# A float32 matmul with bias and residual: bias by a late VectorE shuffle, dense dummy products, finer last stores, and one store cut into 108 and 20 rows

## The chip, the cores and the metric

The kernel runs on one core of a Trainium2 chip. Times are device microseconds (us) of that core; where the text says "span", it means the time from the first to the last instruction in the profile, which is about 2 us shorter. Most runs agree within 0.3%, so a difference of a few tenths of a microsecond needs several rounds. The rounds were spread over five chips, so kernels of different rounds are best compared by their ratio to the kernel before, which ran beside them.

## The reference

```python
# x [16, 512, 1024], weight [1024, 768], bias [768], residual [16, 512, 768], all float32
def reference(x, weight, bias, residual):
    return (np.matmul(x, weight) + bias + residual).astype(np.float32)
```

The 8192 rows of x are 64 tiles of 128 rows. Eight tiles make a super tile, which is loaded and stored in transfers of up to 4 MB; a partition holds eight consecutive rows, so every transfer has long runs per partition. A whole transfer has 128 partitions; where this text speaks of the rows of a transfer, as in "a cut at row 108", it means these partitions. Altogether 87 MB cross the DMA queue.

## The kernel before

x is cast to bf16 on ScalarE, transposed on TensorE, copied out of PSUM by VectorE, multiplied, and added to the residual (to which GpSimd has already added the bias). One in-order queue on SyncE issues nearly all transfers, in the order of a list. These parts matter here (cut):

```python
WARM = 10
HEAD_ORDER = [('bias',), ('warm', 10), ('cast', 0, 'v'), ('cast', 1, 's'), ('tr', 0), ('tr', 1), ...]
ORDER = [('x', 0, 0, 2), ('w', 0, 0, 2), ('x', 0, 2, 4), ('w', 1, 0, 2), ('w', 2, 0, 2), ('w', 3, 0, 2),
 ('x', 0, 4, 6), ('x', 0, 6, 8), ('r', 0, 0, 5), ('x', 1, 0, 4), ('r', 0, 5, 8), ('r', 1, 0, 5),
 ('x', 1, 4, 8), ...                                   # x, w, r: loads; (kind, super tile, first, last)
 ('s', 4, 0, 8), ('s', 5, 0, 8), ('s', 6, 0, 8), ('s', 7, 0, 5), ('s', 7, 5, 7), ('s', 7, 7, 8)]   # stores
...
# a store: all 128 partitions, tiles j0 to j1
nc.sync.dma_start(out=out_d[S, :, j0:j1, :], in_=R[S % RO_SLOTS][:, j0:j1, :])
...
# the bias on all partitions: a product of a row of ones with the bias row, in fp32
nc.tensor.matmul(bias_ps[:, n0:n0 + nl], lhsT=ones_row, rhs=bias_row[:, n0:n0 + nl], ...)
nc.vector.tensor_copy(out=bias_sb, in_=bias_ps)
...
for t in range(HEAD, n_t):          # the steady loop
    cast(t + 2); transp(t + 1)      # ScalarE; TensorE and VectorE
    ... 16 products of tile t ...
    finish(t - 1)                   # VectorE: PSUM + residual
```

## Time and profile before

Three runs took 211.27, 211.29 and 211.53 us. The first lines of the profile's page: busy time of each engine with its share of the span, and what the DMA queues moved. PE stands for TensorE's matmuls, PEld for its weight loads, DVE for VectorE, ACT for ScalarE and POOL for GpSimd; x1308 is a count of instructions.

```profile
span 209.6 us, 3135 instructions
...
PE 204.3 (97%) x1308; PEld 133.6 (64%) x1308; DVE 104.7 (50%) x139; ACT 68.0 (32%) x68; POOL 114.6 (55%) x70
...
DMA packets 5200, 87.23 MB, mean 416 GB/s; under 512 B 577, under 2 KB 577, under 8 KB 1346
## 3 DMA queue, kind: packets, MB, share of 16 engines
q1 hardware_dynamic: 5184, 87.03, 97.6%
q8 instruction: 10, 0.16, 0.3%
```

Two things are full at once: PE (TensorE's matmuls) for 97% of the span, and the DMA queue q1, whose packets take 97.6% of the time of 16 DMA engines. The ten "instruction" packets of queue q8 are 0.3% of the DMA time.

The head, from the timeline (start, duration, engine, line, what, and in brackets the idle time before and what ended it):

```profile
3.30 2.92 PE L196 MATMUL psum_o<-bias_row,ones_row 1*128 1x512 f32 x4
...
5.53 1.04 ACT L131 CAST xb<-x_tile 128x1024 bf16<-128x1024 f32 x1 [2.78 <-DMA x_tile<-in_x_dram]
...
6.26 0.96 DVE L200 COPY bias_sb<-psum_o 128x768 f32<-128x768 f32 x1 [5.12 <-PE psum_o L196]
7.13 0.68 DVE L131 CAST xb<-x_tile 128x1024 bf16<-128x1024 f32 x1
...
10.82 2.11 PE L146 MATMUL psum_o<-w_sb,xt 128*128 128x512 bf16 x8
```

The fp32 bias products hold PE from 3.30 to 6.22 us, and the bias copy holds VectorE until 7.22, so the cast of tile 0 there starts only at 7.13 (the two records overlap by 0.09 us) though its x landed at 5.53. The first real product starts at 10.82.

ScalarE's casts of super tile 1 (tiles 8 to 11, then 12 to 14 in this window), and PE's transposes of tiles 8 and 12:

```profile
31.32 3.89 ACT L131 CAST xb<-x_tile 128x1024 bf16<-128x1024 f32 x4 [8.74 <-DMA x_tile<-in_x_dram]
43.61 2.94 ACT L131 CAST xb<-x_tile 128x1024 bf16<-128x1024 f32 x3 [8.41 <-DMA x_tile<-in_x_dram]
```

```profile
32.88 0.60 PE L139 MATMUL pt<-ident,xb 128*128 128x128 f32 x4
...
45.03 0.60 PE L139 MATMUL pt<-ident,xb 128*128 128x128 f32 x4
```

A cast takes 1.04 us. So tile 8 is ready at 32.36 and is transposed at 32.88; tile 12 is ready at 44.65 and is transposed at 45.03. From there on x is early.

The tail, as busy time in stretches. The last two columns are the mean share of busy DMA engines and what they moved.

```profile
core 0: us, PE busy (x) PEld busy (x) DVE busy (x) ACT busy (x) POOL busy (x), PEclk, DMA share, GB/s
194.00:197.00 3.00, 3.00 (x22) 1.96 (x21) 1.56 (x2) 0.00 (x0) 0.00 (x0) 1.00 1.03 440
197.00:200.00 3.00, 3.00 (x22) 1.96 (x21) 1.55 (x2) 0.00 (x0) 0.00 (x0) 1.00 0.52 217
200.00:203.00 3.00, 3.00 (x22) 1.96 (x21) 1.56 (x2) 0.00 (x0) 0.00 (x0) 1.00 0.98 415
203.00:206.00 3.00, 2.70 (x17) 1.41 (x15) 1.92 (x3) 0.00 (x0) 0.00 (x0) 1.00 0.77 323
```

PE ends at 205.70 us. The queue is not full here any more on average (217 GB/s at 197 to 200 us).

The trace also has a record of every DMA packet. A transfer of 128 rows leaves 16 packets of 4 bytes, one at the end of each engine's share (the semaphore; 578 in this trace), so one can see when each of the 16 engines was done. The records name no engine: where this text follows one, it goes by packets that start within 0.02 us of the end of another. For three transfers (worked out from these records, us):

```
transfer                  first engine done   last engine done   spread
x of tiles 6 and 7                    19.55              19.97     0.42
x of tiles 8 to 11                    29.03              30.79     1.76
store of super tile 6                197.09             200.82     3.74
```

A single engine is behind in the second line. At 20.89 us a 16 KB instruction packet takes 1.10 us, and the 15,360-byte packet that follows takes 1.04 instead of 0.58: 1.56 us lost on one engine. Such packets come every 20 us or so; when the spread grew again, from 2.53 to 3.73 us at about 177 us, one had again just gone by (176.63).

### The profile page before, as it was taken

The numbers are of one execution on the slowest core, as the hardware profiler recorded it, in microseconds if no ns is written. First come the engines' busy times: TensorE is split into PE (matmuls) and PEld (weight loads), VectorE is DVE, ScalarE is ACT, GpSimd is POOL, SyncE is SP. The second block draws the span as 40 slices with busy tenths as digits, with TensorE's granted clock in tenths as the row PEclk, the third lists the DMA queues.
The fourth block names the chain that finished last, engine by engine and source line by source line (L and its number), as shares of the span: only waits on it lengthen the run. The fifth ranks groups of instructions, "written<-read, shape, count | busy, mean of one in ns | idle before, by whom it ended". The sixth has DMA issues, their size and how long they took to land.

```text
span 209.6 us, 3135 instructions
## 1 busy us (share of the span) xinstructions
PE 204.3 (97%) x1308; PEld 133.6 (64%) x1308; DVE 104.7 (50%) x139; ACT 68.0 (32%) x68; POOL 114.6 (55%) x70
## 2 busy tenths in 40 slices
PE   7999999999999999999999999999999999999992
PEld 4756666666666666666666666666666666666661
DVE  0473643474375455455544554554455445545542
ACT  2445307060733053323432152330533134321000
POOL 1000099995278980199599702994059910799000
PEclk9999999999999999999999999999999999999999
DMA  6999999999999999999999999999999999999785
GB/s 236 425 434 436 427 403 448 456 406 404 462 450 402 417 441 425 421 458 400 436 458 422 425 403 436 446 441 419 427 427 446 425 413 435 432 419 441 336 379 231
DMA packets 5200, 87.23 MB, mean 416 GB/s; under 512 B 577, under 2 KB 577, under 8 KB 1346
## 3 DMA queue, kind: packets, MB, share of 16 engines
q1 hardware_dynamic: 5184, 87.03, 97.6%
q8 instruction: 10, 0.16, 0.3%
q14 instruction: 4, 0.03, 0.0%
q10 hardware_dynamic: 2, 0.00, 0.0%
HBM read 61.87 MB, written 25.17 MB: 415 GB/s over the span
## 4 chain that ended last, share of the span: by engine, by line
PE 97%; DVE 1%; issue 0%
PE psum_o L146 79%; PE pt L139 14%; PE psum_o L210 1%; PE psum_o L196 1%; PE psum_o L244 1%; PE psum_o L191 1%; DVE xt L140 0%; DVE ro L248 0%; DVE warm L185 0%
## 5 line engine op out<-in xcount | busy, mean ns | idle before, releaser
L146 PE MATMUL psum_o<-w_sb,xt 128*128 128x512 bf16 x1008 | 174.7, 327 | 0.3 <-DVE xt L140 0.3
L146 PEld LDWEIGHTS <-xt 128*128 128x128 bf16 x1008 | 98.8, 98 | 59.1 <-DVE xt L140 0.6
L171 POOL TENSOR_TENSOR ro<-ro,bias_sb 128x768 f32<-128x768 f32 x58 | 103.2, 1818 | 53.5 <-DMA ro<-in_residual_dram 53.5
L131 ACT CAST xb<-x_tile 128x1024 bf16<-128x1024 f32 x62 | 63.2, 1044 | 116.4 <-PE pt L139 58.6
L140 DVE COPY xt<-pt 128x1024 bf16<-128x1024 bf16 x64 | 44.1, 691 | 79.0 <-PE pt L139 78.9
L181 DVE TENSOR_TENSOR ro<-psum_o,ro 128x768 f32<-128x768 f32 x57 | 54.2, 950 | 12.0 <-POOL ro L171 10.9
L139 PE MATMUL pt<-ident,xb 128*128 128x128 f32 x256 | 39.0, 277 | 0.0
L139 PEld LDWEIGHTS pt<-ident,xb 128*128 128x128 f32 x256 | 30.7, 143 | 7.3
L167 POOL TENSOR_TENSOR ro<-ro 128x768 f32<-128x768 f32 x6 | 10.8, 1814 | 25.2 <-DMA ro<-in_residual_dram 25.2
L177 DVE TENSOR_TENSOR ro<-psum_o,bias_sb 128x768 f32<-128x768 f32 x6 | 5.6, 950 | 3.5 <-PE psum_o L146 3.5
L216 ACT CAST w_sb<-ro 128x768 bf16<-128x768 f32 x4 | 3.3, 832 | 3.8 <-DMA ro<-in_weight_dram 3.8
L200 DVE COPY bias_sb<-psum_o 128x768 f32<-128x768 f32 x1 | 1.0, 958 | 5.1 <-PE psum_o L196 5.1
L210 PE MATMUL psum_o<-warm 128*128 128x256 bf16 x14 | 3.4, 416 | 0.0
L191 PE MATMUL psum_o<-warm 128*128 128x256 bf16 x10 | 2.3, 418 | 1.1 <-DVE warm L185 1.1
L196 PE MATMUL psum_o<-bias_row,ones_row 1*128 1x512 f32 (+1 forms) x4 | 2.9, 880 | 0.0
L210 PEld LDWEIGHTS <-warm 128*128 128x128 bf16 x14 | 1.9, 142 | 1.4 <-issue 0.7
L244 PE MATMUL psum_o<-w_sb,xt 128*128 128x512 bf16 (+1 forms) x16 | 2.8, 326 | 0.0
L191 PEld LDWEIGHTS <-warm 128*128 128x128 bf16 x10 | 1.3, 144 | 1.5 <-DVE warm L185 1.1
L244 PEld LDWEIGHTS <-xt 128*128 128x128 bf16 x16 | 1.6, 98 | 1.1
L196 PEld LDWEIGHTS psum_o<-bias_row,ones_row 1*128 1x128 f32 x4 | 1.2, 318 | 1.5 <-issue 1.5
L216 DVE CAST w_sb<-ro 128x768 bf16<-128x768 f32 x4 | 2.0, 553 | 0.0
L188 ACT ACT_TABLE_LOAD x1 | 1.3, 1283 | 1.3 <-PEq L266 1.3
(12 smaller groups left out, 4.0 us busy)
## 6 DMA issues: line engine op xcount, KB each, us to landing
x_tile<-in_x_dram SPq DMA_DIRECT2D x6, 4096.0 KB, 29.8
out_dram<-ro SPq DMA_DIRECT2D x7, 3072.0 KB, 24.7
ro<-in_residual_dram SPq DMA_DIRECT2D x6, 3072.0 KB, 21.3
x_tile<-in_x_dram SPq DMA_DIRECT2D x4, 1024.0 KB, 8.2
x_tile<-in_x_dram SPq DMA_DIRECT2D x2, 2048.0 KB, 25.9
ro<-in_residual_dram SPq DMA_DIRECT2D x2, 1920.0 KB, 22.1
ro<-in_weight_dram SPq DMA_DIRECT2D x4, 768.0 KB, 10.2
ro<-in_residual_dram SPq DMA_DIRECT2D x2, 1152.0 KB, 28.6
```

The costliest lines, as they stand in the source:

```text
L131: K_((nc.scalar.copy if how == "s" else nc.vector.tensor_copy)(out=dst, in_=src))
L139: K_(nc.tensor.transpose(out=pt[:, q, :], in_=words[:, ts(q, P)], identity=ident))
L140: K_(nc.vector.tensor_copy(out=XT[t % XT_N].rearrange("p q m e -> p (q m e)"), in_=pt.rearrange("p q m -> p (q m)").bitcast(BF16),))
L146: K_(nc.tensor.matmul(PO[t % HEAD][:, n0:n0 + nl], lhsT=XT[t % XT_N][:, q, :, e], rhs=w_sb[:, q, e, n0:n0 + nl], start=(q == 0 and e == 0) ...
L167: K_(nc.gpsimd.tensor_add(out=r, in0=r, in1=tmp(t)))
L171: K_(nc.gpsimd.tensor_add(out=r, in0=r, in1=bias_sb))
L177: K_(nc.vector.tensor_add(out=tmp(t), in0=p, in1=bias_sb))
L181: K_(nc.vector.tensor_add(out=row(t), in0=p, in1=row(t)))
L191: K_(nc.tensor.matmul(PO[0][:, 0:256], lhsT=warm[:, 0:P], rhs=warm, start=True, stop=True))
L196: K_(nc.tensor.matmul(bias_ps[:, n0:n0 + nl], lhsT=ones_row, rhs=bias_row[:, n0:n0 + nl], start=True, stop=True,))
L210: K_(nc.tensor.matmul(PO[1][:, 0:256], lhsT=warm[:, 0:P], rhs=warm, start=True, stop=True))
L244: K_(nc.tensor.matmul(p[:, 0:nl], lhsT=XT[t % XT_N][:, q, :, e], rhs=w_sb[:, q, e, n0:n0 + nl], start=(q == 0 and e == 0), stop=(q == n_q ...
```

## The change

Its intent: start the steady loop earlier (the bias no longer comes through PE and PSUM, the dummy products before the first real ones, meant to bring the full TensorE clock earlier, are twice as wide, the casts of the head are shared by two engines), and end earlier (smaller last stores, the last tile in two pieces). The cut of three tiles at row 108 shifts bytes from some DMA engines to others.

```diff
--- before.py
+++ after.py
@@ -10,29 +10,30 @@
 FP32 = mybir.dt.float32
 BF16 = mybir.dt.bfloat16
 P = 128
+QUAD = 32
 J = 8
 X_SLOTS = 2
 RO_SLOTS = 4
 HEAD = 3
 XT_N = 4
 XB_N = 4
-WARM = 10
+WARM = 12
 EARLY_END = 6
 TMP_SLOT = {0: 3}
 ADDS = [6, 0, 7, 8, 1, 9, 2, 10, 3, 11, 4, 12, 5, 13, 14, 15]
-HEAD_ORDER = [('bias',), ('warm', 10), ('cast', 0, 'v'), ('cast', 1, 's'), ('tr', 0), ('tr', 1),
- ('wc', 0, 0, 's'), ('wc', 0, 1, 'v'), ('warm', 4), ('mm', 0, 0), ('mm', 1, 0),
- ('cast', 2, 'v'), ('cast', 3, 's'), ('tr', 2), ('tr', 3), ('wc', 1, 0, 's'), ('wc', 1, 1, 'v'),
- ('mm', 2, 0), ('mm', 0, 1), ('mm', 1, 1), ('mm', 2, 1), ('wc', 2, 0, 's'), ('wc', 2, 1, 'v'),
- ('mm', 0, 2), ('mm', 1, 2), ('mm', 2, 2), ('wc', 3, 0, 's'), ('wc', 3, 1, 'v'),
- ('cast', 4, 's'), ('mm', 0, 3), ('mm', 1, 3), ('mm', 2, 3)]
-ORDER = [('x', 0, 0, 2), ('w', 0, 0, 2), ('x', 0, 2, 4), ('w', 1, 0, 2), ('w', 2, 0, 2), ('w', 3, 0, 2),
- ('x', 0, 4, 6), ('x', 0, 6, 8), ('r', 0, 0, 5), ('x', 1, 0, 4), ('r', 0, 5, 8), ('r', 1, 0, 5),
- ('x', 1, 4, 8), ('x', 2, 0, 8), ('r', 1, 5, 8), ('r', 2, 0, 8), ('x', 3, 0, 8), ('s', 0, 0, 8),
- ('r', 3, 0, 8), ('x', 4, 0, 8), ('r', 4, 0, 8), ('s', 1, 0, 8), ('x', 5, 0, 8), ('r', 5, 0, 8),
- ('s', 2, 0, 8), ('x', 6, 0, 8), ('r', 6, 0, 8), ('s', 3, 0, 8), ('x', 7, 0, 8), ('r', 7, 0, 8),
- ('s', 4, 0, 8), ('s', 5, 0, 8), ('s', 6, 0, 8), ('s', 7, 0, 5), ('s', 7, 5, 7),
- ('s', 7, 7, 8)]
+HEAD_ORDER = [('cast', 0, 'v'), ('cast', 1, 's'), ('tr', 0), ('tr', 1), ('wc', 0, 0, 's'), ('wc', 0, 1, 'g'),
+ ('warm', 3), ('mm', 0, 0), ('mm', 1, 0), ('cast', 2, 'sv'), ('cast', 3, 'sv'), ('warm', 3),
+ ('tr', 2), ('tr', 3), ('wc', 1, 0, 's'), ('wc', 1, 1, 'v'), ('mm', 2, 0), ('mm', 0, 1),
+ ('mm', 1, 1), ('mm', 2, 1), ('wc', 2, 0, 's'), ('wc', 2, 1, 'v'), ('mm', 0, 2), ('mm', 1, 2),
+ ('mm', 2, 2), ('wc', 3, 0, 's'), ('wc', 3, 1, 'v'), ('bias',), ('cast', 4, 'sv'), ('mm', 0, 3),
+ ('fin', 0), ('mm', 1, 3), ('mm', 2, 3)]
+ORDER = [('x', 0, 0, 2), ('w', 0, 0, 2), ('x', 0, 2, 4), ('w', 1, 0, 2), ('b', 0, 0, 0), ('w', 2, 0, 2),
+ ('w', 3, 0, 2), ('x', 0, 4, 6), ('x', 0, 6, 8), ('r', 0, 0, 5), ('x', 1, 0, 4), ('r', 0, 5, 8),
+ ('r', 1, 0, 5), ('x', 1, 4, 8), ('x', 2, 0, 8), ('r', 1, 5, 8), ('r', 2, 0, 8), ('x', 3, 0, 8),
+ ('s', 0, 0, 8), ('r', 3, 0, 8), ('x', 4, 0, 8), ('r', 4, 0, 8), ('s', 1, 0, 8), ('x', 5, 0, 8),
+ ('r', 5, 0, 8), ('s', 2, 0, 8), ('x', 6, 0, 8), ('r', 6, 0, 8), ('s', 3, 0, 8), ('x', 7, 0, 8),
+ ('r', 7, 0, 8), ('s', 4, 0, 8), ('s', 5, 0, 8), ('s', 6, 0, 5), ('s', 6, 5, 8, 108),
+ ('s', 7, 0, 4), ('s', 7, 4, 6), ('s', 7, 6, 7), ('c', 7, 7, 0), ('c', 7, 7, 1)]
 
 
 @with_exitstack
@@ -75,10 +76,9 @@
     PT = fixed(ps, "pt", 2, [P, n_q, P], FP32)
     (w_sb,) = fixed(sb, "w_sb", 1, [P, n_q, 2, N], BF16)
     (bias_sb,) = fixed(sb, "bias_sb", 1, [P, N], FP32)
-    (bias_row,) = fixed(sb, "bias_row", 1, [1, N], FP32)
-    (ones_row,) = fixed(sb, "ones_row", 1, [1, P], FP32)
+    (bias_row,) = fixed(sb, "bias_row", 1, [P, N], FP32)
     (ident,) = fixed(sb, "ident", 1, [P, P], FP32)
-    (warm,) = fixed(sb, "warm", 1, [P, 256], BF16)
+    (warm,) = fixed(sb, "warm", 1, [P, 512], BF16)
     (warm_a,) = fixed(sb, "warm_a", 1, [1, 2], FP32)
     K_ = tc.keep_in_program_order
     w_st = R[1]
@@ -88,8 +88,10 @@
 
     def pump():
         while queue:
-            kind, S, j0, j1 = queue[0]
-            if kind == "w":
+            kind, S, j0, j1, *cut = queue[0]
+            if kind == "c":
+                need = [("outc", j1)]
+            elif kind in ("w", "b"):
                 need = []
             elif kind == "x":
                 need = [("cast", J * (S - X_SLOTS) + j) for j in range(j0, j1)] if S >= X_SLOTS else []
@@ -104,6 +106,12 @@
             if not all(n in done for n in need):
                 return
             queue.pop(0)
+            if kind == "b":
+                K_(nc.sync.dma_start(
+                    out=bias_row.rearrange("(g p) n -> g p n", p=QUAD)[:, 0, :],
+                    in_=bias[None, :].to_broadcast([P // QUAD, N]),
+                ))
+                continue
             if kind == "w":
                 K_(nc.sync.dma_start(out=w_st[:, 2 * S + j0:2 * S + j1, :], in_=w_d[:, S, j0:j1, :]))
                 continue
@@ -112,7 +120,14 @@
             elif kind == "r":
                 K_(nc.sync.dma_start(out=R[S % RO_SLOTS][:, j0:j1, :], in_=res_d[S, :, j0:j1, :]))
             else:
-                K_(nc.sync.dma_start(out=out_d[S, :, j0:j1, :], in_=R[S % RO_SLOTS][:, j0:j1, :]))
+                n0, nl = (0, N) if kind == "s" else chunks[j1]
+                j1 = j1 if kind == "s" else j0 + 1
+                edges = [0, *cut, P]
+                for p0, p1 in zip(edges, edges[1:]):
+                    K_(nc.sync.dma_start(
+                        out=out_d[S, p0:p1, j0:j1, n0:n0 + nl],
+                        in_=R[S % RO_SLOTS][p0:p1, j0:j1, n0:n0 + nl],
+                    ))
                 done.update(("store", S, j) for j in range(j0, j1))
             done.update((kind, J * S + j) for j in range(j0, j1))
 
@@ -181,23 +196,16 @@
             K_(nc.vector.tensor_add(out=row(t), in0=p, in1=row(t)))
             mark("out", t)
 
-    K_(nc.scalar.dma_start(out=bias_row, in_=bias[None, :]))
     K_(nc.vector.memset(warm, 0.0))
-    K_(nc.vector.memset(ones_row, 1.0))
+    K_(nc.gpsimd.memset(bias_row, 0.0))
     K_(nc.vector.memset(warm_a, 0.0))
     K_(nc.scalar.copy(out=warm_a, in_=warm_a))
     make_identity(nc, ident)
     for _ in range(WARM):
-        K_(nc.tensor.matmul(PO[0][:, 0:256], lhsT=warm[:, 0:P], rhs=warm, start=True, stop=True))
+        K_(nc.tensor.matmul(PO[0][:, 0:512], lhsT=warm[:, 0:P], rhs=warm, start=True, stop=True))
 
     def bias_rows():
-        bias_ps = PO[HEAD - 1]
-        for n0, nl in chunks:
-            K_(nc.tensor.matmul(
-                bias_ps[:, n0:n0 + nl], lhsT=ones_row, rhs=bias_row[:, n0:n0 + nl],
-                start=True, stop=True,
-            ))
-        K_(nc.vector.tensor_copy(out=bias_sb, in_=bias_ps))
+        K_(nc.vector.stream_shuffle(out=bias_sb, in_=bias_row, mask=[0] * QUAD))
 
     pump()
     for kind, *a in HEAD_ORDER:
@@ -205,9 +213,11 @@
             bias_rows()
         elif kind == "cast":
             cast(*a)
+        elif kind == "fin":
+            finish(a[0])
         elif kind == "warm":
             for _ in range(a[0]):
-                K_(nc.tensor.matmul(PO[1][:, 0:256], lhsT=warm[:, 0:P], rhs=warm, start=True, stop=True))
+                K_(nc.tensor.matmul(PO[HEAD - 1][:, 0:512], lhsT=warm[:, 0:P], rhs=warm, start=True, stop=True))
         elif kind == "tr":
             transp(a[0])
         elif kind == "wc":
@@ -222,7 +232,8 @@
                     mm(a[0], n0, nl, a[1], e)
     pump()
     for t in range(HEAD - 1):
-        finish(t)
+        if ("fin", t) not in done:
+            finish(t)
         pool_adds(t)
 
     for t in range(HEAD, n_t):
@@ -246,6 +257,7 @@
                     start=(q == 0 and e == 0), stop=(q == n_q - 1 and e == 1),
                 ))
         K_(nc.vector.tensor_add(out=row(t, n0, nl), in0=p[:, 0:nl], in1=row(t, n0, nl)))
+        mark("outc", chunks.index((n0, nl)))
     mark("out", t)
     pump()
     assert not queue, queue
```

## The prediction

> **What bounds the kernel now.** Profile span 209.6 us, measured 211.29. Two resources are full: the matmul engine (PE busy 204.3 us, 97% of the span and of the chain that ended last) and the DMA queue (97.6% of 16 engines, first page). In the timeline PE turns over one tile each 3.035 us from 20.6 us to 205.7 us without a gap, so only the head, the tail and the room between DMA and PE can change.
>
> **Head.** The clock record gives PE full clock only at about 12.1 us: dummies of 256 columns take 0.24 us, the fp32 bias products hold PE from 3.30 to 6.22 us. The bias copy (6.26, 0.96 us) makes VectorE cast x tile 0 at 7.13 although x landed at 5.53; first real product at 10.82. The change removes both, and a denser warm-up should bring full clock by 5 to 8 us. Following landings from the waits (x 5.53, w 7.4, x 9.9, w 11.8/13.7/15.5, x 18.1) I get the first product at 8.3, the three head tiles done near 18.6 instead of 20.6, tile 3 starting near 19.5 instead of 21.2 (it waits for the first PSUM evacuation). Gain at this point: 1.6 us. The shuffle is an estimate: about 1 us, like the copy of the same 128x768 (0.96), at 16 us, where VectorE has room. POOL's weight cast is off the path.
>
> **Most of that is given back.** The second super tile's halves land at 31.32 and 43.61 us (ScalarE waits for DMA x). The cast takes 1.04 us, so tiles 8 and 12 are castable at 32.36 and 44.65; PE transposes them at 32.88 and 45.03. The slack is only about 0.5 and 0.4 us. DMA is saturated here (425 to 439 GB/s in the windows), and the load order is unchanged. So PE will wait about 1.3 us before tile 8, and the head is worth about 0.3 us. After that slack is larger (2.7 us at tile 16, over 6 later) and PE runs as before.
>
> **Tail.** DMA runs dry unevenly: by the trace's packets, super tile 6's store ends between 197.1 and 200.8 us on the 16 engines. The slowest two are then busy nearly without a break to the end of the data at 208.2 us: the rest (15360-byte packets 0.576 us, 6144 0.234, 3072 0.124, eight each) sums to 7.5 us. The Trainium skill, "DMA: Bandwidth & Descriptors", "Why a DMA increments its semaphore by 16 and not by 1", says the engine count is the largest k up to 16 dividing the slowest dimension, the lowest-numbered engines: 108 rows go to 12, 20 rows to 10. So engines 12 to 15 skip eight 9216-byte packets (0.351 us each, 2.8 us), engines 0 to 9 take three more (1.05 us). No run yet shows which engines lag; if the last four do, the worst one is helped by about 0.8 us. Finer stores leave a last piece of 1 KB rows (about 0.4 us data instead of 1.0), issued 0.3 us earlier. Last data: about 207.5 instead of 208.2.
>
> **Sum:** 211.3 minus 0.7 = 210.6 us, range 209.8 to 211.3. Faster by over 2%: 0.02; within 2%: 0.97; slower: 0.01.
>
> **What shows it:** clock full before 8 us; first product near 8.3; a PE wait of 1 us or more near 31 to 33 us, released by the cast behind x; from tile 12 on PE only 0.2 to 0.4 us earlier; narrower spread of engine end times after super tile 6's store; last data 0.5 to 0.9 us earlier.
>
> **What would make it wrong:** x(1) landing earlier or later (then the head gain grows towards 1.6 us or vanishes); the slow DMA engines being among the first twelve, then the tail loses up to 1 us; a shuffle far dearer than a copy; a slow small-packet tail.

## The result and the profile after

The changed kernel took 217.2, 211.9, 211.56 and 212.02 us. The first is slow (granted clock 0.95, against 0.997 to 1.000 in the other three) and is left out. Beside them the kernel before took 211.27 to 211.58 us in four runs. The other three are 1.0019 times the kernel before, with a 95% interval of 1.0000 to 1.0039. A ratio in this document is the mean time of one kernel's fast runs over that of the other's in the same rounds, so it isn't quite the ratio of the medians. The prediction, 210.6 with a range up to 211.3, is wrong: the change doesn't gain 0.7 us but loses 0.3 to 0.5.

The profile taken with the result fell in the slow run, so the lines below are from a later run of the same code (the first experiment). They answer to those of before. The page (PE's count is a little short: some matmul records are missing in this trace):

```profile
span 209.8 us, 3100 instructions
...
PE 201.3 (96%) x1273; PEld 130.1 (62%) x1298; DVE 104.7 (50%) x140; ACT 67.7 (32%) x69; POOL 116.0 (55%) x72
...
DMA packets 5644, 87.24 MB, mean 416 GB/s; under 512 B 634, under 2 KB 762, under 8 KB 1662
## 3 DMA queue, kind: packets, MB, share of 16 engines
q1 hardware_dynamic: 5630, 87.05, 97.9%
q8 instruction: 10, 0.16, 0.3%
```

The span is 209.8 us, and the DMA queue is as full as before. The head:

```profile
5.76 1.05 ACT L146 CAST xb<-x_tile 128x1024 bf16<-128x1024 f32 x1 [3.54 <-DMA x_tile<-in_x_dram]
5.76 0.69 DVE L146 CAST xb<-x_tile 128x1024 bf16<-128x1024 f32 x1 [4.64 <-DMA x_tile<-in_x_dram]
...
8.53 1.46 PE L161 MATMUL psum_o<-w_sb,xt 128*128 128x512 bf16 x8
...
16.25 1.02 DVE L208 STREAM_SHUFFLE bias_sb<-bias_row 128x768 f32<-128x768 f32 x1
...
19.68 0.48 PE L161 MATMUL psum_o<-w_sb,xt 128*128 128x512 bf16 x2
```

Here the prediction held. The first product is at 8.53 (predicted 8.3), the shuffle takes 1.02 us, tile 3 starts at 19.68 (predicted 19.5; before 21.17). Then super tile 1:

```profile
31.77 3.89 ACT L146 CAST xb<-x_tile 128x1024 bf16<-128x1024 f32 x4 [8.97 <-DMA x_tile<-in_x_dram]
44.04 2.94 ACT L146 CAST xb<-x_tile 128x1024 bf16<-128x1024 f32 x3 [8.38 <-DMA x_tile<-in_x_dram]
```

```profile
32.87 0.66 PE L154 MATMUL pt<-ident,xb 128*128 128x128 f32 x4 [1.32 <-ACT xb L146]
...
45.14 0.66 PE L154 MATMUL pt<-ident,xb 128*128 128x128 f32 x4
```

PE waits 1.32 us before tile 8, as predicted, and now x itself lands 0.4 us later than in the trace of before. At tile 12 PE is 0.1 us behind the kernel before (in the traces of e2 and e4, below, 0.1 and 0.03 us ahead). The whole head gain of 1.5 us is gone, with no 0.3 us left over. The tail:

```profile
core 0: us, PE busy (x) PEld busy (x) DVE busy (x) ACT busy (x) POOL busy (x), PEclk, DMA share, GB/s
194.00:197.00 3.00, 3.00 (x22) 1.97 (x21) 1.55 (x2) 0.00 (x0) 0.00 (x0) 1.00 0.91 381
197.00:200.00 3.00, 2.95 (x21) 1.97 (x21) 1.55 (x2) 0.00 (x0) 0.00 (x0) 1.00 1.03 335
200.00:203.00 3.00, 3.00 (x22) 1.97 (x21) 1.56 (x2) 0.00 (x0) 0.00 (x0) 1.00 0.86 365
203.00:206.00 3.00, 2.87 (x18) 1.56 (x16) 1.75 (x3) 0.00 (x0) 0.00 (x0) 1.00 0.94 386
```

PE ends at 205.86. From 197 to 200 us the DMA engines are busy all the time (share 1.03), yet move only 335 GB/s. In the kernel before the same share moved 440 (194 to 197 us). The last data lands at 208.48 us; before, at 208.23.

### The profile page after: what moved, and what is told of

Same layout as the page of the kernel before. It is cut to its first block, busy times and chain, and to the rows that moved or that the text cites. A ratio compares the mean times of both kernels' runs of the same rounds, so it can differ in the third digit from the quotient of the medians.

```text
span 215.1 us, 3125 instructions
## 1 busy us (share of the span) xinstructions
PE 208.7 (97%) x1298; PEld 132.9 (62%) x1298; DVE 104.6 (49%) x140; ACT 68.2 (32%) x69; POOL 116.1 (54%) x72
## 4 chain that ended last, share of the span: by engine, by line
PE 83%; DMA 14%; ACT 0%; SPq 0%; DVE 0%; issue 0%; ACTq 0%
PE psum_o L161 70%; DMA x_tile<-in_x_dram 14%; PE pt L154 12%; PE psum_o L255 1%; ACT xb L146 0%; DVE ro L259 0%; SPq L116 0%; SPq L119 0%; ACTq L146 0%
## 5 line engine op out<-in xcount | busy, mean ns | idle before, releaser
L161 PE MATMUL psum_o<-w_sb,xt 128*128 128x512 bf16 x1008 | 180.3, 334 | 0.4 <-DVE xt L155 0.3
L161 PEld LDWEIGHTS <-xt 128*128 128x128 bf16 x1008 | 100.5, 100 | 62.8 <-DVE xt L155 0.7
L146 ACT CAST xb<-x_tile 128x1024 bf16<-128x1024 f32 x60 | 61.7, 1045 | 118.9 <-PE pt L154 81.4
L205 PE MATMUL psum_o<-warm 128*128 128x512 bf16 x12 | 4.5, 557 | 1.2 <-DVE warm_a L201 1.2
L205 PEld LDWEIGHTS <-warm 128*128 128x128 bf16 x12 | 1.5, 135 | 3.7 <-issue 2.4
L226 POOL CAST w_sb<-ro 128x768 bf16<-128x768 f32 x1 | 0.8, 822 | 5.5 <-DMA ro<-in_weight_dram 5.5
L146 DVE CAST xb<-x_tile 128x1024 bf16<-128x1024 f32 x1 | 0.7, 694 | 4.4 <-DMA x_tile<-in_x_dram 4.4
L143 ACT CAST xb<-x_tile 128x512 bf16<-128x512 f32 x3 | 1.8, 619 | 3.4 <-DMA x_tile<-in_x_dram 3.4
L144 DVE CAST xb<-x_tile 128x512 bf16<-128x512 f32 x3 | 1.2, 424 | 2.6 <-DMA x_tile<-in_x_dram 2.6
L255 PEld LDWEIGHTS <-xt 128*128 128x128 bf16 x16 | 1.6, 100 | 1.2
L220 PE MATMUL psum_o<-warm 128*128 128x512 bf16 x6 | 1.7, 388 | 0.0
L259 DVE TENSOR_TENSOR ro<-psum_o,ro 128x512 f32<-128x512 f32 (+1 forms) x2 | 1.1, 558 | 1.0 <-PE psum_o L255 0.8
```

The costliest lines, as they stand in the source:

```text
L143: K_(nc.scalar.copy(out=dst[:, 0:K // 2], in_=src[:, 0:K // 2]))
L146: K_((nc.scalar.copy if how == "s" else nc.vector.tensor_copy)(out=dst, in_=src))
L161: K_(nc.tensor.matmul(PO[t % HEAD][:, n0:n0 + nl], lhsT=XT[t % XT_N][:, q, :, e], rhs=w_sb[:, q, e, n0:n0 + nl], start=(q == 0 and e == 0) ...
L205: K_(nc.tensor.matmul(PO[0][:, 0:512], lhsT=warm[:, 0:P], rhs=warm, start=True, stop=True))
L226: K_(copy(out=w_sb[:, q, e, :], in_=w_st[:, 2 * q + e, :]))
L255: K_(nc.tensor.matmul(p[:, 0:nl], lhsT=XT[t % XT_N][:, q, :, e], rhs=w_sb[:, q, e, n0:n0 + nl], start=(q == 0 and e == 0), stop=(q == n_q ...
```

## The experiments

Eighteen kernels ran, all timed against the kernel before in the same rounds. "Uncut" means the changed kernel with the three tiles of super tile 6 stored by one transfer of 128 rows. Medians and ratios:

| run | what | median us | ratio to before | 95% interval |
|---|---|---|---|---|
| e1_after_again | the change | 211.87 | 1.0015 | 1.0002 to 1.0027 |
| e2_head_only | new head, old stores | 211.46 | 0.9997 | 0.9985 to 1.0009 |
| e3_tail_only | old head, new stores | 211.89 | 1.0033 | 1.0006 to 1.0059 |
| e4_after_uncut | uncut | 211.13 | 0.9986 | 0.9971 to 1.0002 |
| e5_cut_96_32 | cut at row 96 | 212.79 | 1.0069 | 1.0052 to 1.0086 |
| e6_cut_one_tile | cut on one tile | 211.05 | 0.9988 | 0.9976 to 1.0000 |
| e7_x1_early | uncut, x earlier | 211.31 | 0.9991 | 0.9979 to 1.0003 |
| e8_x1_early_less | the same, fewer bytes | 210.23 | 0.9948 | 0.9936 to 0.9960 |
| e9_cut_120_8 | cut at row 120 | 212.23 | 1.0065 | 1.0036 to 1.0094 |
| e10_both | e6 and e7 | 211.86 | 1.0026 | 1.0010 to 1.0042 |
| e11_half_products | uncut, half the products | 210.23 | 0.9954 | 0.9942 to 0.9966 |
| e12_cut_mid | uncut, store 3 cut at 96 | 214.03 | 1.0145 | 1.0118 to 1.0173 |
| e13_cut_mid_64 | uncut, store 3 cut at 64 | 216.42 | 1.0229 | 1.0215 to 1.0243 |
| e14_cut_load | uncut, a load cut at 96 | 219.50 | 1.0373 | 1.0359 to 1.0387 |
| e15_mid_by_tile | uncut, store 3 in two by tiles | 211.67 | 1.0003 | 0.9991 to 1.0016 |
| e16_uncut_again | uncut | 211.41 | 0.9992 | 0.9980 to 1.0005 |
| e17_one_tile_again | cut on one tile | 211.18 | 0.9987 | 0.9975 to 1.0000 |
| e18_old_head_uncut | old head, uncut stores | 211.17 | 0.9982 | 0.9968 to 0.9996 |

### Which half of the change loses

My first theory (A): the head is worth nothing and the tail loses. The rival (B): the dense dummies cost clock.

e1_after_again is the change unedited.

> The changed kernel again, to get a profile in the fast state. Theory A (the head gain is eaten by the wait for x at tiles 8 and 12, and the finer tail gives something back the wrong way): span 209.8 us, 211.6 to 212.0 us, and in the trace PE ends at 205.4 to 205.8 but the last data lands as late as before, 208.2 to 208.5. Theory B (the clock is granted a little less than full after the dense warm-up): the tile period is above the 3.035 us of before, PE ends after 205.7, and one run in four or so is in the slow state again.

Measured: 211.87 us, span 209.8, PE ends at 205.86. Six runs, all fast. The tile period is still 3.035 us (transposes at 39.00 and 42.04, for instance), so theory B falls for the fast state. The record of full clock begins at 6.8 us in this trace (12.1 before), which had no effect on the end. In the other traces of the fast state it begins at 3.8 to 6.8 us with the new head and at 10.7 and 11.1 us with the old one (e18, e3); whether the denser dummies or the missing fp32 products do that was not separated.

e2_head_only keeps the new head and takes the old stores:

```diff
- ('s', 6, 0, 5), ('s', 6, 5, 8, 108), ('s', 7, 0, 4), ('s', 7, 4, 6), ('s', 7, 6, 7), ('c', 7, 7, 0), ('c', 7, 7, 1)
+ ('s', 6, 0, 8), ('s', 7, 0, 5), ('s', 7, 5, 7), ('s', 7, 7, 8)
```

> New head (shuffle, dense dummies), old stores. Theory A: 211.1 to 211.5 us, as before, because x of super tile 1 lands at 31.3 to 31.6 whatever the head does. Theory B: 211.7 to 212.1, and the slow state appears here too, because it comes with the head.

Measured: ratio 0.9997. The new head is worth nothing that these rounds can show (the interval is 0.12% to either side), and does no harm.

e3_tail_only is the kernel before with the new list of stores.

> Old head (bias by fp32 products, 256-column dummies), new stores with the 108/20 cut. Theory A: if the tail is what loses, 211.6 to 212.0; my prediction's own step would have it at 210.7 to 210.9. Theory B: 210.7 to 211.0, and no slow run.

Measured: 1.0033, two of its six runs at 213.1 and 213.2 us. The loss is in the tail.

e4_after_uncut takes the cut out of the tail:

```diff
- ('s', 6, 5, 8, 108)
+ ('s', 6, 5, 8)
```

> The changed kernel with the three tiles of super tile 6 stored whole (128 rows, one transfer). If the cut helps the lagging DMA engines as predicted, this is 0.3 to 0.8 us slower than the changed kernel and its engines end super tile 6 over 3 us apart; if the cut loads the wrong engines, it is 0.2 to 0.8 us faster.

Measured: 0.9986, 0.7 us faster than the change beside it. The expectation's second branch holds: the cut itself loses. My prediction had it gain. The same stretches of the tail, uncut:

```profile
194.00:197.00 3.00, 3.00 (x23) 1.97 (x21) 1.55 (x2) 0.00 (x0) 0.00 (x0) 1.00 0.96 410
197.00:200.00 3.00, 2.95 (x21) 1.97 (x21) 1.56 (x2) 0.00 (x0) 0.00 (x0) 1.00 1.03 432
200.00:203.00 3.00, 3.00 (x22) 1.95 (x21) 1.55 (x2) 0.00 (x0) 0.00 (x0) 1.00 0.65 274
203.00:206.00 3.00, 2.72 (x18) 1.43 (x15) 1.89 (x3) 0.00 (x0) 0.00 (x0) 1.00 0.94 380
```

At 197 to 200 us there is the same DMA share as with the cut, and 432 GB/s instead of 335. So the cut didn't only move bytes between engines; it made the packets slow.

### Uneven engines, or slow packets

From the packet records of 189 to 205 us, all those that took over 0.1 us more than usual for their size:

```
run                   slow packets   time over usual, us   mean of 9216-byte packets, us
e4 uncut                         2                   0.8                           0.351
e1 cut at 108                   24                  11.8                           0.402
e5 cut at 96                    28                  11.7                           0.422
e9 cut at 120                   19                   9.4                           0.390
```

The prediction had set each of these packets at 0.351 us. By the rule of the Trainium skill ("DMA: Bandwidth & Descriptors", "Why a DMA increments its semaphore by 16 and not by 1"), the largest number up to 16 that divides the rows, 108 rows go to 12 engines and 20 rows to 10. The trace agrees: the cut kernel has 134 semaphore packets after 189 us and the uncut one 128, and 134 - 128 is just 12 + 10 in place of 16. My hope for the worst engine came true as well: by this rule, which gives the lowest-numbered engines, it was one of the last four. In e1 the slowest engine ends its part of the five-tile store at 198.046 us and goes on at 198.048 with a packet of super tile 7, so it had no rows of the cut store (the same is seen in e3, at 198.30). And still the end was later.

Theory C says that the imbalance costs (ten engines with 11 rows instead of 8). Theory D says that packets get slow whenever an engine doesn't get the rows that it gets in a whole transfer.

e5_cut_96_32 is balanced: both parts spread over 16 engines.

```diff
- ('s', 6, 5, 8, 108)
+ ('s', 6, 5, 8, 96)
```

> The changed kernel, but the three tiles cut at row 96: both transfers spread over 16 engines (6 and 2 rows each), so no engine gets more bytes than another. Theory C (uneven rows: ten engines with 11 rows instead of 8 are what costs): as the uncut kernel, 211.0 to 211.3 us, and the 9216-byte packets keep 0.35 us each. Theory D (a cut that breaks the eight-row groups makes packets slow, whatever the balance): 211.6 to 212.0, with many 9216- and 12288-byte packets 0.3 to 1.3 us over their usual time between 195 and 201 us.

Measured: 212.79 us, 1.5 us above the upper end of what C said, and 0.8 above what D said. C falls: with no imbalance at all the cut is worse than at 108. Slow packets are there as D expected, and the 144 semaphore packets after 189 us show that each of the two parts ran on 16 engines.

e6_cut_one_tile cuts a third of the bytes:

```diff
- ('s', 6, 5, 8, 108)
+ ('s', 6, 5, 7), ('s', 6, 7, 8, 108)
```

> The 108/20 cut on one tile of super tile 6 alone (3072-byte rows): engines 0 to 9 gain 0.37 us, 12 to 15 lose 1.0 us. Theory C: a third of the imbalance, so between the uncut 211.13 and the changed 211.87, or even 0.1 to 0.3 faster than uncut, because the worst engine (one of the last four, by the trace) is helped and the others have that much room. Theory D: slow packets again, 211.4 or more.

Measured: 0.9988, as uncut. Six slow packets, 1.8 us over in sum. In this trace the last data lands at 207.70 us instead of 208.10, and in the repeats (e17, e16) at 208.06 instead of 208.39, so the worst engine seems to be relieved; the times don't show it beyond their scatter.

e9_cut_120_8 cuts at row 120 (15 engines, then 8).

```diff
- ('s', 6, 5, 8, 108)
+ ('s', 6, 5, 8, 120)
```

> The changed kernel, cut at row 120 instead of 108: 15 engines[...], then one more row each for eight engines. Theory D (packets get slow when an engine's rows are no longer its usual group of eight): hardly any slow 9216-byte packets but for the last eight rows, and 210.9 to 211.3 us, as uncut. If any cut of these rows costs, whatever the grouping: 211.6 or more.

Measured: 1.0065, with slow packets already at 194.9 us, before the eight last rows could begin (135 semaphore packets after 189 us: 15 and 8 engines, as supposed). So the hypothesis as I had put it is wrong, or fifteen engines don't get the rows that I supposed: I assumed blocks of eight consecutive rows without having checked it, and no record here shows which engine gets which row.

### Is the cut slow in the middle, for loads, and by which property

e12_cut_mid leaves the tail uncut and cuts the 3 MB store of super tile 3:

```diff
- ('s', 3, 0, 8)
+ ('s', 3, 0, 8, 96)
```

> Uncut at the end, but the whole store of super tile 3, in the middle of the run, cut at row 96 (6 and 2 rows per engine, balanced). Theory D: slow 24576-byte packets between 150 and 175 us, and at least 0.7 us lost at the end: 211.8 to 213. If slow packets come only from the tail's mix of stores: 211.0 to 211.3, as uncut.

e13_cut_mid_64 cuts it at 64 instead.

```diff
- ('s', 3, 0, 8)
+ ('s', 3, 0, 8, 64)
```

> Uncut at the end, the store of super tile 3 cut in two halves of 64 rows (16 engines, four rows each). If the eight-row grouping matters: slow 24576-byte packets between 150 and 165 us as with the cut at 96, and 212.5 us or more. If only row counts that are no power of two matter: no slow packets and 211.0 to 211.3.

e15_mid_by_tile makes two transfers of it without a cut in rows:

```diff
- ('s', 3, 0, 8)
+ ('s', 3, 0, 4), ('s', 3, 4, 8)
```

> Uncut, the store of super tile 3 in two transfers of four tiles with all 128 rows each. If two transfers in place of one were the cause: slow packets and 212 us or more. I expect 211.0 to 211.3 and no more slow packets than in the uncut kernel.

e14_cut_load cuts a load, the residual of super tile 6, at 96.

```diff
- ('r', 6, 0, 8)
+ ('r', 6, 0, 8, 96)      # issued in a loop over the two parts, like the stores
```

> Uncut stores, the load of residual 6 cut at row 96. If loads suffer like stores: slow 24576-byte packets between 143 and 160 us, 212.5 us or more. If only stores do: 211.0 to 211.4.

Measured: 1.0145, 1.0229, 1.0003 and 1.0373. Two stretches, 150 to 157 and 157 to 164 us, of five kernels. First uncut, then the store in two by tiles:

```profile
150.00:157.00 7.00, 6.95 (x47) 4.55 (x47) 3.60 (x5) 2.13 (x3) 3.33 (x2) 1.00 1.01 435
157.00:164.00 7.00, 6.95 (x48) 4.79 (x48) 3.11 (x4) 2.09 (x2) 7.00 (x5) 1.00 1.01 432
```

```profile
150.00:157.00 7.00, 6.95 (x46) 4.58 (x46) 3.67 (x5) 2.19 (x3) 3.06 (x2) 1.00 1.00 425
157.00:164.00 7.00, 6.95 (x48) 4.75 (x48) 3.11 (x4) 2.09 (x2) 7.00 (x5) 1.00 1.04 445
```

Store cut at 96, store cut at 64, load cut at 96:

```profile
150.00:157.00 7.00, 6.95 (x47) 4.55 (x47) 3.47 (x5) 2.09 (x2) 3.16 (x2) 1.00 1.05 411
157.00:164.00 7.00, 6.95 (x48) 4.68 (x47) 3.12 (x5) 2.09 (x2) 7.00 (x5) 1.00 0.96 355
```

```profile
150.00:157.00 7.00, 6.95 (x46) 4.60 (x46) 3.70 (x5) 2.23 (x3) 3.06 (x2) 1.00 1.03 372
157.00:164.00 7.00, 6.95 (x48) 4.72 (x47) 3.11 (x4) 2.09 (x2) 7.00 (x5) 1.00 1.01 282
```

```profile
150.00:157.00 7.00, 6.95 (x47) 4.56 (x46) 3.77 (x5) 3.31 (x4) 0.00 (x0) 1.00 1.05 221
157.00:164.00 7.00, 6.95 (x48) 4.69 (x48) 2.52 (x4) 2.09 (x2) 2.12 (x2) 1.00 0.91 339
```

The DMA share stays near 1 in all of them while GB/s falls, to 282 with the halves and to 221 with the load. Two transfers instead of one cost nothing (e15, whose 0.3 us over expectation is within the scatter of e16 below). A power of two doesn't help (e13 is the worst store). Loads suffer more than stores: the median 24,576-byte packet of e14 between 142 and 162 us took 1.72 us, against 0.91 uncut. What is shown, then: on this queue, which is nearly full, cutting a 128-row transfer of three to eight tiles by rows makes its packets, and those of transfers beside it, slow, for loads and stores, balanced or not. With one tile cut there were only two to four slow packets more than uncut (e6, e17).

A cause that fits is in the Trainium skill. "SBUF — State Buffer", "Door 1: The DMA port swizzle", says that DMA bandwidth depends on how many of 16 ports the partitions reach, and that rows 0 to 63 reach 8. "DMA: Bandwidth & Descriptors", "The descriptor swizzle", says that in a 128-partition transfer each engine writes to one port, a different one for each. A cut by rows could put several engines on one port. At 64 it must, if the skill is right: 16 engines would share the 8 ports of each half, and this store was the slowest. This is argued, not shown: the records have no engine or port number. It would also explain e9, if 15 engines share ports; that, too, is open. And it doesn't say why, with the same cut at 96, the load lost 3.7% and the store 1.5%. A rival that no run tests is the other end of the transfers: a cut by rows also changes which addresses of the tensors in HBM are in flight together.

### What sets the end

Theory E: the head gain is eaten only by the wait for x. Theory F: the worst DMA engine is busy from the first packet to the last, so an earlier PE can't help.

e7_x1_early moves x of super tile 1 ahead of residual 0 in the uncut kernel, and gives tiles 6 and 7 the path of tiles 0 to 5, which finish without their residual:

```diff
-EARLY_END = 6
+EARLY_END = 8
+AFTER = {5: 9, 6: 10, 7: 11}      # and pool_adds skips t while AFTER[t] is not yet added
-ADDS = [6, 0, 7, 8, 1, 9, 2, 10, 3, 11, 4, 12, 5, 13, 14, 15]
+ADDS = [0, 1, 2, 3, 4, 8, 9, 5, 10, 6, 11, 7, 12, 13, 14, 15]
- ('r', 0, 0, 5), ('x', 1, 0, 4), ('r', 0, 5, 8), ('r', 1, 0, 5), ('x', 1, 4, 8), ('x', 2, 0, 8)
+ ('x', 1, 0, 4), ('r', 0, 0, 5), ('x', 1, 4, 8), ('r', 1, 0, 5), ('r', 0, 5, 8), ('x', 2, 0, 8)
```

> Uncut, with the loads of x for super tile 1 moved ahead of residual 0 (and all eight first tiles finished without their residual). Theory E (the head gain is eaten only by the wait for x at tiles 8 and 12): PE no longer waits there, PE ends 1.0 to 1.4 us earlier (204.5 to 204.9), and the time falls as much, to 209.8 to 210.2. Theory F (the worst DMA engine is busy from the first packet to the last, so the end cannot move with PE): PE ends about a us earlier, but the last data still lands at 207.9 to 208.2 and the time is 210.9 to 211.2, as uncut.

Measured: 0.9991. ScalarE's casts of tiles 8 and 12 in e7:

```profile
26.95 3.89 ACT L147 CAST xb<-x_tile 128x1024 bf16<-128x1024 f32 x4 [4.34 <-DMA x_tile<-in_x_dram]
36.44 2.94 ACT L147 CAST xb<-x_tile 128x1024 bf16<-128x1024 f32 x3 [5.61 <-DMA x_tile<-in_x_dram]
```

x is now 4.6 and 7.5 us earlier than in the uncut kernel (e4: 31.51 and 43.90), and the wait at tile 8 is gone. PE loses part of it between tiles 12 and 13, where it waits for VectorE's copies, and ends at 205.02 instead of 205.72. The last data lands at 208.37 us, no earlier than uncut. The time doesn't move. E falls. The semaphores show where the end lies: the last of the 16 engines are done at 208.14 and 208.37 us, ten of them by 207.00.

e8_x1_early_less also leaves out 393 KB of loads. Its output is wrong, which doesn't matter for the time.

```diff
- ('r', 7, 0, 8)
+ ('r', 7, 0, 7)
```

> As the kernel before it, and the residual of the last tile is not loaded (393 KB less, 0.98 us of every DMA engine; the last tile is wrong on purpose). Theory F: now 0.8 to 1.0 us faster than with the load, 210.0 to 210.3. Theory E: the same as with the load, within 0.2 us.

Measured: 0.9948 against 0.9991, or 0.9 us, which is what those bytes take on every engine. PE's work is unchanged. F holds.

e11_half_products leaves out half the products of the steady loop. Its output is wrong, which doesn't matter for the time.

```diff
-                for e in range(2):
-                    for n0, nl in chunks:
-                        mm(t, n0, nl, q, e)
+                for n0, nl in chunks:
+                    mm(t, n0, nl, q, 0, q == n_q - 1)      # the last one stops the sum
```

> Uncut, with half the products of the middle tiles left out (wrong on purpose): PE has about 90 us less to do, and half as many instructions to fetch. Theory F: PE is not what sets the end. The time falls by no more than 1 to 2.5 us, to 208.6 to 210.2: the engines that served two 16 KB instruction packets serve one, so their spread at the last big store falls from 3.5 to under 2.5 us. If PE set the end, it falls by tens of us or at least by 3.

Measured: 0.9954. The first lines of its page:

```profile
span 208.4 us, 2148 instructions
...
PE 138.9 (67%) x803; PEld 88.2 (42%) x818; DVE 104.7 (50%) x140; ACT 65.9 (32%) x69; POOL 115.9 (56%) x72
```

PE is busy for 65 us less than in the kernel before (138.9 against 204.3; I had expected 90), and the kernel is 1.0 us faster (0.7 to 0.8 against uncut). One reason for 65 instead of 90 is that the granted clock falls to half in some stretches (29.3 to 36.1 us, for instance; 0.865 in the mean), in which the same products take longer (at 33.4 us eight of them took 2.77 us, as long as sixteen at full clock). The spread of the engines at the last 3 MB store is 2.65 us, against 3.55 uncut with twice the products; I had expected under 2.5. There are six 16 KB instruction packets instead of ten; that the engines furthest behind had served two of them before was my supposition, which the records can't settle. PE, busy for 97% of the span and on the chain of waits for as long, is not what ends this kernel: with half the products gone the end hardly moves.

e10_both joins the edits of e6 and e7.

> x of super tile 1 early, and the 108/20 cut on one tile only. Theory F: the end is set by the worst DMA engine, which the small cut moved to 207.7 us; with PE about 0.5 us earlier the last pieces can follow, so 210.5 to 210.9. If PE or the last store's issue were the bound, the same gain; if the cut was luck, 211.1 to 211.3.

Measured: 1.0026. Two runs at 210.93 and 211.07 us, four from 211.75 to 212.24. The profile caught the fastest (span 208.7, last data at 207.29). Why most runs were slower is open; the expectation is missed.

### Is there a version that beats both

e16 and e17 are the code of e4 and of e6 again. e18 is the code of e3 with e4's edit, that is the old head and the new stores, uncut.

> Uncut again: 211.0 to 211.3 us, 0.2 to 0.4 under the kernel before, if the finer stores alone are a gain. If the first result was luck: as before.

> Cut of one tile again: if shared ports cost in proportion to the bytes cut, this is within 0.2 us of uncut, not better by more: 211.0 to 211.4.

> Old head, new stores uncut. If the new head is worth nothing because the worst DMA engine sets the end: the same as e16 within 0.2 us. If the new head is worth the 0.3 us that I predicted: 0.3 slower than e16.

Measured: 0.9992, 0.9987 and 0.9982. e18 needs nothing of the new head and is as fast as any: 0.18% under the kernel before, with an interval that excludes 1. Uncut with the new head came out at 0.9986 and 0.9992. So the finer last stores gain 0.2 to 0.4 us (of the three intervals only e18's excludes 1), the head nothing, and the cut on one tile nothing that these rounds can show.

## Why the prediction was wrong

- **The head, up to tile 3: right.** First product at 8.53 (predicted 8.3), tile 3 at 19.68 (19.5), the shuffle 1.02 us (about 1).
- **"Most of that is given back": right, and more so.** PE waits 1.32 us before tile 8 (predicted about 1.3). The remainder, "the head is worth about 0.3 us", measured nothing (e2: 0.9997). There are two reasons. In the traces of the new head x lands 0.1 to 0.4 us later (31.44, 31.51 and 31.77 in e2, e4 and e1, against 31.32; why is open), so that PE ends at 205.64 to 205.86 instead of 205.70. And even 0.7 us off the end of PE, in e7, doesn't move the end.
- **The finer stores: right in kind.** Without the cut they gain 0.2 to 0.4 us (e18, e4, e16).
- **The step that failed: "So engines 12 to 15 skip eight 9216-byte packets (0.351 us each, 2.8 us)", and from it "the worst one is helped by about 0.8 us".** I carried 0.351 us over from transfers of 128 rows (in the kernel before, loads; in e4 the whole store has the same mean) to transfers of 108 and 20. The count of engines was right and the worst engine was, as I had only hoped, among those helped, but the packets became slower: 24 of them took 11.8 us longer in sum, which is 0.7 us for each of 16 engines. Cut against uncut in the same rounds, the ratios 1.0015 and 0.9986 differ by 0.6 us in the wrong direction. My list of what could go wrong had "the slow DMA engines being among the first twelve"; the engines were where I hoped, and the packets were what went wrong.
- **The bound.** I counted PE's end and the last store's issue as setting the end, next to the DMA tail. e8 and e11 show that in the uncut kernel DMA sets it. That it is the engine furthest behind is read from the packet records: in the kernel before one engine ends super tile 6's store at 200.83 us, the packets of super tile 7 take 8 x (0.576 + 0.234 + 0.124) = 7.5 us, and the last data lands at 208.23, so this engine had no pause. In that kernel, though, it is nearly a tie: most of the other engines had stood idle for want of a store, the last time until 207.09, when the last store's first packet starts, and all are done at 208.07 to 208.20. The finer stores loosen this: in e4 fourteen engines are done by 207.75 and only two later, at 208.07 and 208.10. So there the engines furthest behind alone set the end, and that would be why the finer stores gained so little.

In sum: predicted -0.3 for the head, which leaves -0.4 of the -0.7 for the tail; measured about 0 for the head, -0.2 to -0.4 for the finer stores, +0.6 for the cut.

What stays open: which port or bank makes the packets of a cut transfer slow; why neighbouring transfers suffer; whether the cause lies on this side or in HBM; e10's two groups of runs; the one slow run (every experiment's runs were fast, so none can say whether it comes with the head).

## What to carry to other kernels

When DMA is near full, as here, keep all 128 partitions in every large transfer, and split it along the free dimension if it must be split: two transfers by tiles cost nothing here, two by rows cost up to 7.9 us for 3 MB. When DMA is near full, look at when each engine finishes, not at the mean share: the engine that is furthest behind can set the end, and work taken off a 97% busy TensorE can be worth nothing. Don't carry a packet's duration from one transfer shape to another.

## What the Trainium skill lacked or had wrong

- "DMA: Bandwidth & Descriptors", "Rules for kernel authors", says of two transfers to disjoint partition halves only that they don't pay ("Don't bother — they serialize"). Here they cost: one 3 MB store in two halves of 64 rows made the kernel 216.4 us, against 211.7 with the same store in two by tiles in the same rounds (e13, e15).
- "SBUF — State Buffer", "Door 1: The DMA port swizzle", has measured bandwidths only for ranges that start at 0 and have a power of two of rows. Not there: what several transfers of other ranges do to each other, as with cuts into 96 and 32, 108 and 20, or 120 and 8, which slowed transfers next to them (12,288-byte packets of other stores took up to 1.3 us longer).
- "Why a DMA increments its semaphore by 16 and not by 1" on the first of these pages gives how many engines a row count uses, with which the trace agrees (22 semaphore packets for 108 and 20 rows), but not which rows each engine gets when there are fewer than 128.
- "Runtime: NRT & Kernel Launch", "Instruction fetch mechanics", doesn't have what fetching instructions costs data transfers: in this kernel each of ten 16 KB packets took about 1.0 us of one DMA engine, the first followed by a data packet 0.46 us over its usual time, and the next load was complete on 15 engines at 24.56 us but on the last at 25.89.
